# State products of the sample streams: four fp32 products of 32 rows at TensorE's row tiles, in place of six full products with masked rows

## The chip, the cores and the metric

The kernel runs on one core of one Trainium2 chip. The metric is the time of one execution in device microseconds, taken as the median of several runs; lower is better. The engines are named as the profile names them: PE is TensorE's matrix product and PEld its weight load, DVE is VectorE, ACT is ScalarE, POOL is GpSimd, and SP is the queue that issues nearly all DMAs. PSUM, where products land, has eight banks of 128 x 512 fp32 values.

## The reference

Two request groups, a prompt of 512 frames and eight sample streams of 16 frames each, pass together through two layers. In each layer a combined projection feeds a gated MLP branch and a gated DeltaNet branch, and an MLP follows. The change lies in the DeltaNet branch, where each of eight heads updates a state S of 128 x 128 per stream:

```
def step(S, xs):
    U_, W_, P_, qg_, kg_, gl_ = xs
    vnew = U_ - jnp.einsum('bhcd,bhde->bhce', W_, S)
    o = jnp.einsum('bhcd,bhde->bhce', qg_, S) + jnp.einsum('bhij,bhje->bhie', P_, vnew)
    S = S * gl_[..., None, None] + jnp.einsum('bhcd,bhce->bhde', kg_, vnew)
    return S, o
```

The prompt has one stream, taken here in four chunks of 128 frames. The samples have eight streams of 16 frames each; together they make one tile of 128 rows, in which stream b owns rows 16 b to 16 b + 15. Their state update is, per stream, the product of 16 rows of `kg` with the same 16 rows of `vnew`: eight results of 128 x 128 a head.

## The kernel before

The activations lie transposed, features on partitions and 640 frames along the free axis. A matrix product with a weight block is written as three products in fp32r: both operands are split into a high part (ScalarE's copy, L133) and a low part (VectorE's subtraction, L134), and high x high, high x low and low x high are summed. A weight block of 128 outputs is thus 16 units of three products of 320 columns; the names `pg_p` and `pg_g` in the profile are their PSUM tiles, `raw`, `whi` and `wlo` the weight block and its parts.

The DeltaNet work of a layer is spread among these units. A layer's head stage has ten slots; slot h takes a list of weight blocks (five of them, 80 units, in slots 2 to 8). Three generators run beside the blocks: `prepare` of head h - 1, `chain` of head h - 2 and `roots` of head h - 3. Each is cut by `yield` into segments, and `paced` spreads them over the slot: a generator of length L whose next segment is due at d is resumed at the first unit u of n for which d n <= u L. `chain` has the length CHAIN, `prepare` the length PREPARE = 70. At each unit `chain` comes first, then `roots`, then `prepare`, then the unit's three products. What is due after the last unit is issued at the end of the slot.

TensorE executes in exactly this program order, written out by hand. The order on the other engines comes from a planner that lists instructions by readiness and priority; `chain` has the highest priority, then `prepare` and the splits of weights.

`chain` (L629 on) does four chunks t of the prompt one after the other: a product with the state (`ps_kS`), VectorE's `y` (L732), a product `ps_w`, ScalarE's copy `w` (L680), and then the state product `ps_S`, the output products `ps_o`, VectorE's new state (L750) and ScalarE's copy `osb` (L684). Its banks have the tag "c". Beside it runs the generator `sample` for the eight streams, with banks of the tag "d", which `prepare` and `roots` use too. Of each tag there are two banks. `prepare` ends with a product of 32 small tiles into a "d" bank, `ps_Z` (L617), and begins in the next slot with transposes into "d" banks, `kt` (L516).

`sample` scales the eight old states by their decays (POOL), computes `w` for all streams, and then forms the eight updates in two halves of four streams. For each half, `w` is masked so that each of four column blocks holds only one stream's rows (`we`: four ScalarE copies for the high part, L717, and one POOL product for the low part, L718), and three products of 128 rows and 512 columns are summed into a "d" bank; VectorE adds the bank to the states (L723). The first half is issued with `ps_w` of chunk 3, the second after the outputs of chunk 3.

Of the kernel before, what the change touches and what calls it, by code (L numbers as in the profile page):

```python
# [9 lines left out]
F32 = mybir.dt.float32  # L10
# [7 lines left out]
P = 128  # L18
# [17 lines left out]

SIDE = (1, 4, 2, 2, 2, 2, 2, 2, 5, 6)

CHAIN, PREPARE, ROOTS, GATING = 66, 70, 26, 48
AHEAD = 200  # L40


def rep(ap, dim, n):

    a = ap.unsqueeze(dim)
    shape = list(a.shape)
    shape[dim] = n
    return a.to_broadcast(shape)
# [14 lines left out]
def encoder(ctx, tc, xin, wblk, wba, sct, sdelta, prow, pcol, gates, wst, bsr, convw, consts, delta0,  # L63
# [68 lines left out]
    def split(dst_hi, dst_lo, src):  # L132
        nc.scalar.activation(dst_hi, src, AF.Copy)  # L133
        nc.vector.tensor_tensor(dst_lo, src, dst_hi.bitcast(F32), op=ALU.subtract)  # L134
# [52 lines left out]
    def bank(tag, nm):  # L187
        return psp.tile([P, 512], F32, tag=tag, name=f"ps_{nm}")
# [440 lines left out]
    def chain(l, h, pl, gate, out):  # L629
        sq, kT, qg, kg, AP_, vn, n0c, QT, S8 = out.pop(h)  # L630
        beta, ngam, egam, dL, dec, rowd = gate
        kb, qb, N1 = kbs[h % 2], qbs[h % 2], n1s[h % 2]
        nm = f"{l}{h}"


        m0c = pl.tile([P, 4, 32], F32, tag="m0c", bufs=1, name=f"m0c{nm}")
        nc.vector.transpose(m0c[:].rearrange("p t n -> p (t n)"), n0c[:, 0:4, :].rearrange("p t n -> p (t n)"))
        M0 = pl.tile([P, 4, 64], F32, tag="M0", bufs=1, name=f"M0{nm}")
        N0 = pl.tile([P, 5, 64], F32, tag="N0", bufs=2, name=f"N0{nm}")
        for dst, src, n in ((M0, m0c, 4), (N0, n0c, 5)):  # L640
            for b in range(2):
                nc.vector.tensor_scalar(dst[:, :, 32 * b:32 * b + 32], src[:, 0:n, :], odd[:, b:b + 1], None, op0=ALU.mult)
        yield 8
        by = bank("c", f"Y{nm}")
        bys = by[:, 0:256].rearrange("p (t n) -> p t n", t=4)
        for t in range(4):
            for hf in halves:
                mm(bys[hf, t, :], QT[hf, t, :], M0[hf, t, :], True, True, pos=(hf.start, hf.start))
        Y = pl.tile([P, 4, 64], F32, tag="Y", bufs=1, name=f"Y{nm}")
        nc.scalar.activation(Y[:], bys, AF.Copy)  # L650
        yield 4
        b1 = bank("c", f"M1{nm}")
        for t in range(4):
            mm(b1[0:64, t * 64:(t + 1) * 64], N0[0:64, t, :], Y[0:64, t, :], True, True)
        M1 = pl.tile([P, 4, 64], F32, tag="M1", bufs=1, name=f"M1{nm}")
        nc.vector.tensor_tensor(M1[0:64], b1[0:64, 0:256].rearrange("p (t n) -> p t n", t=4), M0[0:64], op=ALU.add)
        bz = bank("c", f"Z{nm}")
        bzs = bz[:, 0:256].rearrange("p (t n) -> p t n", t=4)
        for t in range(4):
            for hf in halves:  # L660
                mm(bzs[hf, t, :], Y[hf, t, :], N0[hf, t, :], True, True, pos=(hf.start, hf.start))
        for hf in halves:
            nc.vector.tensor_tensor(N1[hf, :, hf], bzs[hf], N0[hf, 0:4, :], op=ALU.add)
        yield 5
        b2 = bank("c", f"Y2{nm}")
        for t in range(4):
            mm(b2[64:128, t * 64:(t + 1) * 64], AP_[0:64, t, 0, 64:128], M1[0:64, t, :], True, True, pos=(0, 64))
        nc.scalar.activation(M1[64:128].rearrange("p t n -> p (t n)"), b2[64:128, 0:256], AF.Copy)
        yield 4
        b3 = bank("c", f"N2{nm}")  # L670
        for t in range(4):
            mm(b3[0:64, t * 64:(t + 1) * 64], M1[64:128, t, :], N1[64:128, t, 64:128], True, True, pos=(64, 0))
        nc.vector.tensor_copy(N1[0:64, :, 64:128], b3[0:64, 0:256].rearrange("p (t n) -> p t n", t=4))
        yield 4

        osb = pl.tile([P, 5, P], F32, tag="osb", bufs=1, name=f"osb{nm}")

        def copied(ps, tag):
            tl = pl.tile([P, P], F32, tag=tag, bufs=1, name=f"{tag}{nm}")
            nc.scalar.activation(tl[:], ps, AF.Copy)  # L680
            return tl

        def o_done(po, t):
            nc.scalar.activation(osb[:, t, :], po[:, 0:P], AF.Copy)  # L684


        def sample():
            pk = bank("d", f"kS{nm}4")
            pq = bank("d", f"qS{nm}4")
            for ps, buf in ((pk, kb), (pq, qb)):  # L690
                for j in range(2):
                    for c in range(4):
                        mm(ps[32 * c:32 * c + 32, 0:P], buf[:, c, 16 * j:16 * j + 32], S8[:, 2 * c + j, :], j == 0, j == 1, pos=(0, 32 * c))
            y = pl.tile([P, P], F32, tag="y4", bufs=1, name=f"y{nm}4")
            nc.vector.scalar_tensor_tensor(y[:], pk[:, 0:P], egam[:, 4, h:h + 1], vn[:, 4, :], op0=ALU.mult, op1=ALU.add)
            qs = copied(pq[:, 0:P], "qs")
            nc.gpsimd.tensor_tensor(S8[:], S8[:], rep(dec[:, 4:12, h], 2, P), op=ALU.mult)
            yield
            pw = bank("d", f"w{nm}4")
            for hf in halves:  # L700
                mm(pw[hf, 0:P], N0[hf, 4, :], y[hf], True, True, pos=(hf.start, hf.start))
            w = copied(pw[:, 0:P], "w4")
            wp_, kp = (pl.tile([P, 2, P], F32R, tag=tag, name=f"{tag}{nm}") for tag in ("w4p", "k4p"))
            split(wp_[:, 0, :], wp_[:, 1, :], w[:])
            split(kp[:, 0, :], kp[:, 1, :], kg[:, 4, :])
            yield
            po = bank("d", f"o{nm}4")
            mm(po[:, 0:P], w[:], AP_[:, 4, 1, :], True, False)
            mm(po[:, 0:P], qs[:], ident, False, True)
            o_done(po, 4)  # L710
            yield
            Sf = S8[:].rearrange("p b n -> p (b n)")
            for a in range(2):

                we = pl.tile([P, 2, 4, P], F32R, tag="we", name=f"we{nm}{a}")
                for b in range(4):
                    nc.scalar.activation(we[:, 0, b, :], wp_[:, 0, :].bitcast(F32), AF.Copy, scale=maskb[:, 4 * a + b:4 * a + b + 1])  # L717
                nc.gpsimd.tensor_tensor(we[:, 1], rep(wp_[:, 1, :].bitcast(F32), 1, 4), rep(maskb[:, 4 * a:4 * a + 4], 2, P), op=ALU.mult)  # L718
                yield
                pS = bank("d", f"S{nm}4{a}")  # L720
                for i, (u, v) in enumerate(((0, 0), (0, 1), (1, 0))):
                    mm(pS[:], kp[:, u, :], we[:, v].rearrange("p b n -> p (b n)"), i == 0, i == 2)
                nc.vector.tensor_tensor(Sf[:, a * 512:(a + 1) * 512], Sf[:, a * 512:(a + 1) * 512], pS[:], op=ALU.add)  # L723
            nc.sync.dma_start(ds_out[l, :, h].rearrange("b d e -> d b e"), S8[:])

        beside, S = sample(), None
        for t in range(4):
            if t:
                pk = bank("c", f"kS{nm}{t}")
                mm(pk[:, 0:P], kT[:, t, :], S[:], True, True)  # L730
                y = pl.tile([P, P], F32, tag="y", bufs=1, name=f"y{nm}{t}")
                nc.vector.scalar_tensor_tensor(y[:], pk[:, 0:P], egam[:, t, h:h + 1], vn[:, t, :], op0=ALU.mult, op1=ALU.add)  # L732
                if t >= 2:
                    next(beside)
                yield 4
            pw = bank("c", f"w{nm}{t}")
            mm(pw[:, 0:P], N1[:, t, :], y[:] if t else vn[:, 0, :], True, True)
            w = copied(pw[:, 0:P], "w")
            if t:
                next(beside)  # L740
            yield 4
            pS = bank("c", f"S{nm}{t}")
            mm(pS[:, 0:P], kg[:, t, :], w[:], True, True)
            po = bank("c", f"o{nm}{t}")
            mm(po[:, 0:P], w[:], AP_[:, t, 1, :], True, t == 0)
            if t:
                mm(po[:, 0:P], S[:], qg[:, t, :], False, True)
            Sn = pl.tile([P, P], F32, tag="S", bufs=2, name=f"S{nm}{t}")
            if t:
                nc.vector.scalar_tensor_tensor(Sn[:], S[:], dec[:, t, h:h + 1], pS[:, 0:P], op0=ALU.mult, op1=ALU.add)  # L750
            else:
                nc.vector.tensor_copy(Sn[:], pS[:, 0:P])
            S = Sn
            o_done(po, t)
            if t < 3:
                yield 4
        nc.sync.dma_start(dp_out[l, h], S[:])
        run(beside)
        out[h, "o"] = osb, sq
# [611 lines left out]
```

## Time and profile before

| what | value |
|---|---|
| median of 3 runs | 2483.79 us (2483.41 to 2486.56) |
| the profiled execution: its own time | 2483.95 us |
| its span, first to last instruction | 2482.0 us |
| mean granted TensorE clock | 0.993 |
| PE busy | 2424.5 us, 98% |
| DVE, ACT, POOL busy | 60%, 49%, 19% |
| masked copies `we` | 128 on ScalarE, 32 on POOL |
| products `ps_S<-we,k4p` | 96, of 512 columns |

A row of a timeline gives the start in us from the span's start, how long the group lasted, engine, line, operation, the tile written and those read, shape and count; in square brackets, where there are any, stand the engine's idle time before it and what ended it. TensorE's products overlap in their pipeline, so its pace is read from one start to the next. An fp32 product appears as two records.

### The profile page before, as it was taken

The page shows a single profiled execution, that of the slowest core. Times are in us where ns is not written, and L with a number is a line of the kernel's source. Part 1 is how long each engine was busy: PE and PEld are TensorE (multiplying, and loading weights), DVE is VectorE, ACT ScalarE, POOL GpSimd, SP SyncE. Part 2 cuts the span into 40 slices and gives each one's busy share as a digit, 9 for nine tenths or more (in the row PEclk, how much of TensorE's full clock was granted, in tenths as well). Part 3 has the DMA queues.
Part 4 walks back from the last instruction along what each step waited for, and adds up shares of the span by engine and source line. Part 5 has one row for each costly group of instructions (what it writes and reads, how often), then busy time and mean ns, then how long its engine had stood idle before and what let it go on. Part 6 is the DMA issues. An engine that isn't in the chain of part 4 may idle for free. (4 is left out here: it accounts for less than half of the span.)

```text
span 2482.0 us, 44959 instructions
## 1 busy us (share of the span) xinstructions
PE 2424.5 (98%) x18120; PEld 2338.1 (94%) x18120; DVE 1477.9 (60%) x2982; ACT 1212.8 (49%) x2324; POOL 482.1 (19%) x582
## 2 busy tenths in 40 slices
PE   8999999999999999999999999999999999999997
PEld 7999999998999999999999999999989999999997
DVE  6656677536555746556456677664275567556453
ACT  5767676633123625244447676774332245244352
POOL 0223433211222100000213343341112220000002
PEclk9999999999999999999999999999999999999998
DMA  5233333337532222222233333333464322222221
GB/s 175 86 108 115 111 92 95 126 115 243 160 104 77 69 77 85 69 86 77 85 95 117 102 97 97 102 117 114 153 226 139 98 65 81 69 85 77 78 83 61
DMA packets 124495, 261.27 MB, mean 105 GB/s; under 512 B 17232, under 2 KB 57072, under 8 KB 124288
## 3 DMA queue, kind: packets, MB, share of 16 engines
q1 hardware_dynamic: 123968, 257.10, 32.2%
q8 instruction: 142, 2.33, 0.4%
q0 software_dynamic: 320, 1.31, 0.2%
q14 instruction: 65, 0.53, 0.1%
HBM read 218.22 MB, written 40.15 MB: 104 GB/s over the span
## 5 line engine op out<-in xcount | busy, mean ns | idle before, releaser
L133 ACT ACTIVATE whi<-raw 128x1024 fp32r<-128x1024 f32 (+1 forms) x304 | 309.0, 1018 | 630.6 <-PE pg_dn L80 255.4
L134 DVE TENSOR_TENSOR wlo<-raw,whi 128x1024 fp32r<-128x1024 f32 (+1 forms) x304 | 383.7, 1263 | 171.0 <-ACT whi L133 157.2
L80 PE MATMUL pg_dn<-gh,wlo 128*128 128x320 f32 x1024 | 317.3, 310 | 2.1 <-DVE wlo L134 2.1
L80 PE MATMUL pg_dn<-gl,whi 128*128 128x320 f32 x1024 | 316.6, 309 | 0.7 <-DVE gl L1128 0.7
L80 PE MATMUL pg_dn<-gh,whi 128*128 128x320 f32 x1024 | 316.8, 309 | 0.0
L80 PE MATMUL pg_g<-Ah,whi 128*128 128x320 f32 x896 | 289.4, 323 | 1.0 <-ACT sg L830 1.0
L80 PE MATMUL pg_g<-Ah,wlo 128*128 128x320 f32 x896 | 276.8, 309 | 0.0
L80 PE MATMUL pg_g<-Al,whi 128*128 128x320 f32 x896 | 276.4, 308 | 0.0
L80 PE MATMUL pg_p<-Ah,whi 128*128 128x320 f32 x768 | 251.4, 327 | 0.0
L80 PE MATMUL pg_p<-Al,whi 128*128 128x320 f32 x768 | 236.9, 309 | 0.4 <-DVE Al L134 0.4
L80 PE MATMUL pg_p<-Ah,wlo 128*128 128x320 f32 x768 | 237.2, 309 | 0.0
L80 PEld LDWEIGHTS pg_dn<-gh,wlo 128*128 128x128 f32 x1024 | 192.2, 188 | 4.4 <-DVE wlo L134 4.4
L80 PEld LDWEIGHTS pg_dn<-gl,whi 128*128 128x128 f32 x1024 | 192.2, 188 | 1.2 <-DVE gl L1128 1.2
L80 PEld LDWEIGHTS pg_dn<-gh,whi 128*128 128x128 f32 x1024 | 192.2, 188 | 0.0
L80 PEld LDWEIGHTS pg_g<-Ah,whi 128*128 128x128 f32 x896 | 168.6, 188 | 8.7 <-issue 3.5
L1242 DVE TENSOR_TENSOR t<-pg_dn,rateb 128x640 f32<-128x640 f32 x64 | 52.7, 824 | 202.5 <-PE pg_dn L80 202.5
L80 PEld LDWEIGHTS pg_g<-Al,whi 128*128 128x128 f32 x896 | 168.7, 188 | 1.5
L80 PEld LDWEIGHTS pg_g<-Ah,wlo 128*128 128x128 f32 x896 | 168.2, 188 | 0.0
L479 DVE SCALAR_TENSOR_TENSOR yb<-cb,cw,yb 128x664 f32<-128x664 f32 x144 | 138.1, 959 | 27.4 <-ACT yb L477 25.8
L80 PEld LDWEIGHTS pg_p<-Ah,whi 128*128 128x128 f32 x768 | 145.2, 189 | 6.0 <-issue 2.4
L80 PEld LDWEIGHTS pg_p<-Al,whi 128*128 128x128 f32 x768 | 144.7, 188 | 0.7 <-DVE Al L134 0.7
L80 PEld LDWEIGHTS pg_p<-Ah,wlo 128*128 128x128 f32 x768 | 144.2, 188 | 0.0
(748 smaller groups left out, 6245.3 us busy)
## 6 DMA issues: line engine op xcount, KB each, us to landing
raw<-in_wblk SPq DMA_DIRECT2D x304, 512.0 KB, 3.5
gd<-sg SPq DMA_DIRECT2D x56, 320.0 KB, 3.3
rg<-gd SPq DMA_DIRECT2D x44, 320.0 KB, 3.2
S<-in_sdelta SPq DMA_DIRECT2D x16, 512.0 KB, 6.1
out<-S SPq DMA_DIRECT2D x16, 512.0 KB, 3.8
gr<-rowd SPq DMA_DIRECT2D x16, 320.0 KB, 5.2
er<-rowd SPq DMA_DIRECT2D x16, 320.0 KB, 3.9
ond<-osb SPq DMA_DIRECT2D x16, 320.0 KB, 2.2
```

The source lines that it names most:

```text
L80: nc.tensor.matmul(out, lhsT=lhsT, rhs=rhs, start=start, stop=stop, **kw)
L133: nc.scalar.activation(dst_hi, src, AF.Copy)
L134: nc.vector.tensor_tensor(dst_lo, src, dst_hi.bitcast(F32), op=ALU.subtract)
L479: nc.vector.scalar_tensor_tensor(yb[:, 0:CY], cb[:, j:j + CY], cw[:, c, j:j + 1], yb[:, 0:CY], op0=ALU.mult, op1=ALU.add)
L1242: nc.vector.tensor_tensor(t[:], ps[:, :, 0:HT], rate, op=ALU.mult)
```

## The change

The split of `w` and `kg` for the samples goes, and with it the masks by stream. Instead ScalarE writes two copies of `w`, one that keeps the even streams and one that keeps the odd ones (`par` holds one for the rows of even or of odd streams, zero for the others). Rows 32 c to 32 c + 31 hold streams 2 c and 2 c + 1, so four products with 32 rows each, at the row tiles of the array, with 256 columns (even copy, odd copy) give the eight updates in plain fp32. Each of the four writes a bank of its own, two of tag "c" and two of tag "d", and four VectorE additions of 256 columns take them up.

All four products now stand in one last segment of `sample`, which runs after the outputs of chunk 3 and a further `yield 4`. The length CHAIN grows by four to match.

```diff
-CHAIN, PREPARE, ROOTS, GATING = 66, 70, 26, 48
+CHAIN, PREPARE, ROOTS, GATING = 70, 70, 26, 48
...
             w = copied(pw[:, 0:P], "w4")
-            wp_, kp = (pl.tile([P, 2, P], F32R, tag=tag, name=f"{tag}{nm}") for tag in ("w4p", "k4p"))
-            split(wp_[:, 0, :], wp_[:, 1, :], w[:])
-            split(kp[:, 0, :], kp[:, 1, :], kg[:, 4, :])
+
+            w2 = pl.tile([P, 2, P], F32, tag="w2", bufs=1, name=f"w2{nm}")
+            for j in range(2):
+                nc.scalar.activation(w2[:, j, :], w[:], AF.Copy, scale=par[:, j:j + 1])
             yield
             po = bank("d", f"o{nm}4")
             mm(po[:, 0:P], w[:], AP_[:, 4, 1, :], True, False)
             mm(po[:, 0:P], qs[:], ident, False, True)
             o_done(po, 4)
             yield
-            Sf = S8[:].rearrange("p b n -> p (b n)")
-            for a in range(2):
-
-                we = pl.tile([P, 2, 4, P], F32R, tag="we", name=f"we{nm}{a}")
-                for b in range(4):
-                    nc.scalar.activation(we[:, 0, b, :], wp_[:, 0, :].bitcast(F32), AF.Copy, scale=maskb[:, 4 * a + b:4 * a + b + 1])
-                nc.gpsimd.tensor_tensor(we[:, 1], rep(wp_[:, 1, :].bitcast(F32), 1, 4), rep(maskb[:, 4 * a:4 * a + 4], 2, P), op=ALU.mult)
-                yield
-                pS = bank("d", f"S{nm}4{a}")
-                for i, (u, v) in enumerate(((0, 0), (0, 1), (1, 0))):
-                    mm(pS[:], kp[:, u, :], we[:, v].rearrange("p b n -> p (b n)"), i == 0, i == 2)
-                nc.vector.tensor_tensor(Sf[:, a * 512:(a + 1) * 512], Sf[:, a * 512:(a + 1) * 512], pS[:], op=ALU.add)
+            yield
+            yield
+            banks = [bank(tag, f"S{nm}4{c}") for c, tag in enumerate("ccdd")]
+            for c, q in enumerate(quarters):
+                mm(banks[c][:, 0:2 * P], kg[q, 4, :], w2[q].rearrange("p b n -> p (b n)"), True, True, pos=(q.start, 0))
+            for c in range(4):
+                nc.vector.tensor_tensor(S8[:, 2 * c:2 * c + 2, :], S8[:, 2 * c:2 * c + 2, :],
+                                        banks[c][:, 0:2 * P].rearrange("p (b n) -> p b n", b=2), op=ALU.add)
             nc.sync.dma_start(ds_out[l, :, h].rearrange("b d e -> d b e"), S8[:])
...
             o_done(po, t)
-            if t < 3:
-                yield 4
+            yield 4
         nc.sync.dma_start(dp_out[l, h], S[:])
         run(beside)
```

## The prediction

> **What bounds the kernel now.** I read the page first, then the windows of single head slots, then the timelines of TensorE, VectorE and ScalarE around the products that the diff touches.
>
> ```profile
> span 2482.0 us, 44959 instructions
> PE 2424.5 (98%) x18120; PEld 2338.1 (94%) x18120; DVE 1477.9 (60%) x2982; ACT 1212.8 (49%) x2324; POOL 482.1 (19%) x582
> L1242 DVE TENSOR_TENSOR t<-pg_dn,rateb 128x640 f32<-128x640 f32 x64 | 52.7, 824 | 202.5 <-PE pg_dn L80 202.5
> ```
>
> ```profile
> 191.20:243.00 51.80, 51.80 (x478) 48.84 (x478) 35.81 (x116) 36.12 (x89) 20.31 (x30) 1.00 0.34 105
> 243.00:294.80 51.80, 51.80 (x478) 48.84 (x478) 35.99 (x116) 36.12 (x89) 20.34 (x30) 1.00 0.35 106
> ```
>
> The second fence is the windows view: time, then busy time of PE, PEld, DVE, ACT and POOL, then clock and DMA. Two head slots in a row last 51.80 us each with PE busy in all of it, at full granted clock, while DVE and ACT have some 16 us free. So TensorE sets the end of this stage, in the order in which its instructions are written. An edit there is worth what it adds to or takes from TensorE's own time, plus any wait that it plants in TensorE's queue. Busy time does not show short waits (the ends are modelled), so I read start to start.
>
> The sum is made against the profiled execution, 2483.95 us: its span of 2482.0 and 1.95 around it. The median of the runs is 2483.79, 0.16 below.
>
> **Removed: the six products.** First an fp32 product followed by the stream (PE timeline, one piece), then the slot's end with the second stretch of three.
>
> ```profile
> 182.63 0.38 PE L80 MATMUL ps_kS<-S,kT 128*128 128x128 f32 x2
> 182.77 0.39 PE L80 MATMUL pg_g<-Ah,whi 128*128 128x320 f32 x1
> 183.00 0.30 PE L80 MATMUL pg_g<-Al,whi 128*128 128x320 f32 x1
> ```
>
> ```profile
> 188.30 0.38 PE L80 MATMUL ps_S<-w,kg 128*128 128x128 f32 x2
> 188.52 0.39 PE L80 MATMUL ps_o<-AP,w 128*128 128x128 f32 x2
> 188.74 0.39 PE L80 MATMUL ps_o<-qg,S 128*128 128x128 f32 x2
> 188.88 0.95 PE L80 MATMUL ps_S<-we,k4p 128*128 128x512 f32 x3
> 189.67 0.31 PE L80 MATMUL pg_g<-Ah,whi 128*128 128x320 f32 x1
> 189.82 0.31 PE L80 MATMUL pg_g<-Al,whi 128*128 128x320 f32 x1
> 189.97 0.31 PE L80 MATMUL pg_g<-Ah,wlo 128*128 128x320 f32 x1
> 190.21 0.45 PE L80 MATMUL ps_Z<-n0c,y 32*32 32x32 f32 x32
> 190.61 0.66 PE L516 MATMUL ps_kt02a<-cst,kT 128*128 128x128 f32 x4
> 191.17 0.33 PE L516 MATMUL ps_kt02b<-cst,kT 128*128 128x128 f32 x1
> ```
>
> From an fp32 product to the second stream product it takes 183.00 - 182.63 = 0.37 us; with three products of 512 columns between, 189.82 - 188.74 = 1.08. So a stretch costs 0.71, and two stretches in each of 16 heads 22.7 us.
>
> **Added: four fp32 products at row tiles.** No product of the trace uses four row tiles over all 128 columns. The nearest are four column tiles (`ps_kS`, `ps_qS`) and two diagonal tiles of 64 rows (`ps_w<-y,N`).
>
> ```profile
> 219.72 0.62 PE L80 MATMUL ps_qS<-S,qb 128*32 128x128 f32 x16
> 220.27 0.42 PE L80 MATMUL pg_p<-Ah,whi 128*128 128x320 f32 x1
> ```
>
> ```profile
> 225.44 0.38 PE L80 MATMUL ps_kS<-S,kT 128*128 128x128 f32 x2
> 225.75 0.44 PE L80 MATMUL ps_w<-y,N 64*64 64x128 f32 x4
> 226.12 0.42 PE L80 MATMUL pg_g<-Ah,whi 128*128 128x320 f32 x1
> 226.37 0.31 PE L80 MATMUL pg_g<-Al,whi 128*128 128x320 f32 x1
> ```
>
> An fp32 product is two records, and one of 128 columns takes 188.52 - 188.30 = 0.22, so 0.11 a pass. Sixteen records of `ps_qS` fit into 0.55 us where one after the other they would take 1.76: tiles run side by side. The two-tile group costs 226.37 - 225.44 - 0.37 = 0.56, of which two passes are 0.22; 0.34 is the drain in, an uncovered weight load, the drain out and another load. The load back to 128 columns is 226.37 - 226.12 - 0.15 = 0.10, so entering with 128 columns of weights instead of 64 adds 0.05. Two passes of 256 columns are 0.44, and the tiles' starts are spread over 0.02. Sum 0.85 a head, 13.6 us. Upper end: no overlap at all between row tiles, 4 x 0.44 instead of 0.44, 1.30 more a head. Lower end: no fixed cost, 0.44. I take 0.85, because both tiled groups of the trace overlap.
>
> "TensorE: Matmul & The Clock Gate", Part 3, of the Trainium skill gives a measured speedup of 3.07 for four row tiles instead of 4. By that, an estimate, a pass takes 1.30 times as long, 0.13 us a head and 2.1 us in all, and the sum below would end at 2495. No run here shows row tiles of this kind yet.
>
> **Where it stands, and the bank it takes.** In slots 2 to 8 (80 units of three stream products) a segment due at d is issued at unit ceil(80 d / CHAIN). The state products, due at 65 of 66 and now 69 of 70, are at unit 79 in both. One unit later, at the slot's end, `prepare` issues its last product `ps_Z` (L617), which needs a "d" bank. Before, only one "d" bank was in use by then. Now two of the four new banks are "d" and there are only two, so `ps_Z` waits for the third of four VectorE adds, and with it everything that TensorE has behind it: the transposes `kt` and the next slot's stream.
>
> ```profile
> 189.87 0.69 DVE L723 TENSOR_TENSOR S<-S,ps_S 128x512 f32<-128x512 f32 x1 [0.80 <-PE ps_S L80]
> 190.47 0.45 DVE L134 TENSOR_TENSOR k4p<-kg,k4p 128x128 fp32r<-128x128 f32 x1
> 190.84 0.28 DVE L618 TENSOR_TENSOR n0c<-n0c,ps_Z 128x128 f32<-128x128 f32 x1
> ```
>
> Let P be the last stream start ahead of the group. The group starts at P + 0.24 (190.21 - 189.97), its second pass at P + 0.58 (0.22 + 0.10 + 0.02). A 128-column record lasts 0.27 (0.38 less 0.11), so one of 256 lasts 0.38 and ends at P + 0.96. The add follows after 0.04 (188.88 + 0.95 to 189.87). An add of 512 columns lasts 0.69 and the next starts after 0.60; 640 columns last 0.824. So 256 columns last 0.42 and follow each other by 0.33: the third ends at P + 1.00 + 0.66 + 0.42 = P + 2.08, and TensorE goes on 0.05 later (190.56 to 190.61), P + 2.13. Without the wait `ps_Z` would start at P + 0.58 + 0.31 + 0.25 + 0.15 + 0.24 = P + 1.53. The wait is 0.60 in each of 14 heads (slots 2 to 8 of two layers), 8.4 us. Ends: 0 if that bank comes free within the unit, and 1.9 if a 1.23 us VectorE split is put among the adds. "TensorEngine Tiling (Array Packing)", PSUM Bottleneck, of the Trainium skill speaks against the change in the same way: tiling hastens TensorE, not the emptying of PSUM.
>
> A credit: the add after `ps_Z` was held by the split of `k4p` until 190.84, and `kt02b` started 0.18 after the last `kt02a` where 0.11 is its pace; `k4p` goes, so 0.07 x 14 = 1.0 us returns.
>
> **Moved: the chain, earlier by up to four units.** CHAIN 70 puts `kS` of chunk 2 (due 45) at unit 52 instead of 55 and `ps_w` of chunk 2 with the sample's `ps_o` (due 49) at 56 instead of 60. What feeds them on VectorE and ScalarE does not move with them.
>
> ```profile
> 226.40 1.23 DVE L134 TENSOR_TENSOR wlo<-raw,whi 128x1024 fp32r<-128x1024 f32 x1 [2.29 <-ACT whi L133]
> 227.54 0.34 DVE L732 SCALAR_TENSOR_TENSOR y<-ps_kS,cu,vtok 128x128 f32<-128x128 f32 x1
> ```
>
> ```profile
> 223.72 1.28 ACT L499 ACT_TABLE_LOAD   x1 [3.04 <-DVE pr L591]
> 225.33 1.04 ACT L133 ACTIVATE whi<-raw 128x1024 fp32r<-128x1024 f32 x1
> 228.43 0.26 ACT L680 ACTIVATE w<-ps_w 128x128 f32<-128x128 f32 x1
> ```
>
> ```profile
> 228.27 0.31 PE L80 MATMUL pg_g<-Ah,wlo 128*128 128x320 f32 x1
> 228.41 0.38 PE L80 MATMUL ps_w<-y,n 128*128 128x128 f32 x2
> 228.74 0.49 PE L80 MATMUL ps_o<-AP,w 128*128 128x128 f32 x2
> 229.06 0.39 PE L80 MATMUL ps_o<-cst,qs 128*128 128x128 f32 x2
> ```
>
> ```profile
> 1658.81 0.34 DVE L732 SCALAR_TENSOR_TENSOR y<-ps_kS,cu,vtok 128x128 f32<-128x128 f32 x1
> ```
>
> `y` stands behind `wlo`, which waits for `whi`, which stands on ScalarE behind a table load for `E`, which waits for VectorE's substitution of another head. `y` ends at 227.88, half a microsecond before TensorE wants it. Four units earlier (12 products at 13 steps in 1.90 us, 226.37 to 228.27, so 1.76) TensorE is there at 226.65. If the order `E`, `whi`, `wlo`, `y` stays, it waits until 227.94: 1.29 us. The wait for `w` that `ps_o` had (229.06 - 228.41 is 0.65 where four records take 0.44, so 0.21) is swallowed. Net 1.08 a head, in the ten heads with this pattern (slots 3 to 7 of both layers, the first `y` at 227.54, the last at 1658.81): 10.8 us. Ends: 0 if `y` goes ahead of `wlo`, 1.66 if `w`, ending at 228.69, decides (`ps_o` at 228.74 instead of 226.87, less the 0.21).
>
> **Edits at nothing.** ScalarE loses eight masked copies and two splits a head and gets two scaled copies, POOL loses two, VectorE has four shorter adds for two:
>
> ```profile
> L717 ACT ACTIVATE we<-w4p,mis x128: 384/389/410, 176.5 to 1764.9; 128x128 fp32r<-128x128 f32 x128
> L718 POOL TENSOR_TENSOR we<-w4p,mis x32: 1037/1042/1049, 176.8 to 1764.1; 128x512 fp32r<-128x512 f32 x32
> L723 DVE TENSOR_TENSOR S<-S,ps_S x32: 686/689/689, 185.8 to 1767.1; 128x512 f32<-128x512 f32 x32
> ```
>
> ScalarE gives back 6 x 0.39 x 16 = 37 us and POOL 33 us, beside TensorE's stream; VectorE's adds take 4 x 0.42 instead of 2 x 0.69. Were that cover gone, VectorE's 0.3 us a head would cost 5 us. The store of the states is issued on SP's queue after the last add, as before, at about the same time; behind it stand only loads for blocks two ahead. In slot 9 chain and roots now fill 96 of 96 units instead of 92; no `prepare` follows, so no bank wait.
>
> **Sum.** -22.7 + 13.6 + 8.4 - 1.0 + 10.8 = +9.1 on 2483.95: 2493.
>
> **The rivals.** First, no mid-slot wait: scheduling places `y` ahead of `wlo`, or `whi` ahead of `E`. VectorE idles 2.29 us ahead of `wlo`, which speaks for it; against it, the due times move the chain alone, while `E`, `whi` and `wlo` are issued where they were. Then -1.7: 2482.3, no change. Second, on the other side, TensorE's saving stands bare, because the adds of the two "d" banks are done first: `ps_Z` then waits for the first add, P + 1.00 + 0.42 + 0.05 = P + 1.47, before it is due. Its place is the slot's end, its price 8.4 us; with the first rival it gives -10.1, 2474, and it decides once the bank is back by P + 1.53. For it: VectorE idles 0.80 ahead of that add. Against: program order, "c" before "d". Third, the row tiles do not overlap: +20.8, and the bank wait goes since the adds start tile by tile; 2494.7, or 2505.5 with the mid-slot wait. Against it: every tiled group seen overlaps, though each uses other columns.
>
> **How the numbers follow.** Forecast 0.42, first rival 0.27, second 0.22, third 0.09. About 0.2% (5 us) can be told from no change. Slower: forecast and third less a share with a smaller wait, 0.50; within: 0.28; faster: 0.22. The range runs from the second rival, 2474 (2473 with a little for rounding), to the third with the wait, 2506; the forecast's own is 2488 to 2501 (waits of 0.6 to 1.66, bank waits as worked out).
>
> **What would show it.** Products `ps_S<-w2,kg` starting four within 0.03 us and two passes 0.32 apart: tiles overlap. `ps_Z` some 0.6 us late behind the third add: the bank wait. `ps_w` of chunk 2 behind `y` and `wlo` in slots 3 to 7: the mid-slot wait. A slot of 51.80 us becoming 52.8 is the forecast, 51.8 the first rival, 51.2 the second, 52.5 the third. It is wrong if the engines' order changes with the due times.

## The result, and the profile after

The changed kernel takes 2496.07 us (median of 4 runs, 2494.12 to 2499.57) where the kernel before took 2483.73 beside it: ratio 1.0052, 95% interval 1.0038 to 1.0066. The change costs 12.3 us. The forecast was 2493, slower by 9.1. The profiled execution is the slowest of the four (2499.57 us, span 2497.9), so I take from it lengths of slots and of waits, and not the span.

First the page of the kernel after: span, and busy time of the engines.

```profile
span 2497.9 us, 44813 instructions
PE 2419.2 (97%) x18152; PEld 2327.5 (93%) x18152; DVE 1479.8 (59%) x2982; ACT 1164.6 (47%) x2184; POOL 436.8 (17%) x550
```

TensorE's busy time fell by 5.3 us, ScalarE's by 48, POOL's by 45, and the kernel became slower. So the loss lies in TensorE's waits. One head slot in the windows view (from the first transpose `kt` of one slot to that of the next) shows the same:

```profile
192.19:245.21 53.02, 51.27 (x488) 47.99 (x479) 36.37 (x115) 32.90 (x80) 17.00 (x27) 1.00 0.33 102
```

It lasts 53.02 us where the slot before lasted 51.80, and PE is busy for only 51.27 of it: 1.75 us are now idle time that the view can see. Slots 3 to 7 all have this length, to 0.01 us, in both layers. Slot 2 went from 51.17 to 51.99, slot 8 from 51.50 to 51.56, slot 9 from 54.64 to 54.10. Over both layers the slots 2 to 9 add up to +12.5 us, which is the difference of the medians.

The end of a slot, TensorE's timeline of the kernel after:

```profile
189.70 0.31 PE L80 MATMUL pg_g<-Ah,wlo 128*128 128x320 f32 x1
189.94 0.71 PE L80 MATMUL ps_S<-w,kg 32*128 32x256 f32 x8
190.58 0.41 PE L80 MATMUL pg_g<-Ah,whi 128*128 128x320 f32 x1
190.83 0.31 PE L80 MATMUL pg_g<-Al,whi 128*128 128x320 f32 x1
190.98 0.31 PE L80 MATMUL pg_g<-Ah,wlo 128*128 128x320 f32 x1
191.81 0.45 PE L80 MATMUL ps_Z<-n0c,y 32*32 32x32 f32 x32 [0.52 <-DVE S L719]
192.19 0.66 PE L516 MATMUL ps_kt02a<-cst,kT 128*128 128x128 f32 x4
192.69 0.33 PE L516 MATMUL ps_kt02b<-cst,kT 128*128 128x128 f32 x1
```

The four products and their two passes (eight records) start within 0.34 us, and the second stream product behind them follows the last one ahead of them by 190.83 - 189.70 = 1.13; two normal steps are 0.29, so the group costs 0.84. `ps_Z` was due 0.24 after 190.98, at 191.22, and starts at 191.81: 0.59 late, held by `S`. VectorE's timeline there:

```profile
190.67 1.42 DVE L719 TENSOR_TENSOR S<-S,ps_S 128x256 f32<-128x256 f32 x4 [3.06 <-PE ps_S L80]
192.34 0.29 DVE L618 TENSOR_TENSOR n0c<-n0c,ps_Z 128x128 f32<-128x128 f32 x1 [0.25 <-PE ps_Z L80]
```

The four adds start 0.33 apart and last 0.42; the third ends at 190.67 + 0.66 + 0.42 = 191.75, and `ps_Z` starts 0.06 later.

The middle of the slot: TensorE, then VectorE, then ScalarE.

```profile
228.12 0.31 PE L80 MATMUL pg_g<-Ah,wlo 128*128 128x320 f32 x1
229.66 0.46 PE L80 MATMUL ps_w<-y,n 128*128 128x128 f32 x2 [1.23 <-DVE y L729]
...
230.18 0.39 PE L80 MATMUL ps_o<-cst,qs 128*128 128x128 f32 x2
```

```profile
224.93 0.17 DVE L591 TENSOR_TENSOR pr<-Bs,X 128x5 f32<-128x5 f32 x1
...
228.02 1.22 DVE L134 TENSOR_TENSOR wlo<-raw,whi 128x1024 fp32r<-128x1024 f32 x1 [2.46 <-ACT whi L133]
229.16 0.34 DVE L729 SCALAR_TENSOR_TENSOR y<-ps_kS,cu,vtok 128x128 f32<-128x128 f32 x1
```

```profile
225.18 1.28 ACT L499 ACT_TABLE_LOAD   x1 [3.77 <-DVE pr L591]
226.48 0.40 ACT L499 ACTIVATE E<-gr,ngam 128x128 f32<-128x128 f32 x1
...
226.94 1.05 ACT L133 ACTIVATE whi<-raw 128x1024 fp32r<-128x1024 f32 x1
```

`ps_w` of chunk 2 was due one step after 228.12, at 228.27, and starts at 229.66: 1.39 us in which TensorE stands with the stream queued behind it. Read upwards, it is the chain that the prediction named: `y` behind `wlo`, `wlo` waiting for `whi`, `whi` behind the table load and `E`, and that load waiting for the last product `pr` of VectorE's substitution. (The next head's `E` has only one buffer, and the substitution's `Bs` lies in it until `pr` has read it.) Counted from start to start there are 12 such waits of `ps_w` with 14.8 us in all: ten of 1.39 in slots 3 to 7, and two of 0.44 in slot 2, where it is the product of chunk 3.

### The profile page after: what moved, and what is told of

Same layout as the page of the kernel before. It is cut to its first block, busy times and chain, and to the rows that moved or that the text cites. A ratio compares the mean times of both kernels' runs of the same rounds, so it can differ in the third digit from the quotient of the medians.

```text
span 2497.9 us, 44813 instructions
## 1 busy us (share of the span) xinstructions
PE 2419.2 (97%) x18152; PEld 2327.5 (93%) x18152; DVE 1479.8 (59%) x2982; ACT 1164.6 (47%) x2184; POOL 436.8 (17%) x550
## 5 line engine op out<-in xcount | busy, mean ns | idle before, releaser
L479 DVE SCALAR_TENSOR_TENSOR yb<-cb,cw,yb 128x664 f32<-128x664 f32 x144 | 145.2, 1008 | 24.5 <-ACT yb L477 23.3
```

The lines of the kernel that those rows point to most:

```text
L479: nc.vector.scalar_tensor_tensor(yb[:, 0:CY], cb[:, j:j + CY], cw[:, c, j:j + 1], yb[:, 0:CY], op0=ALU.mult, op1=ALU.add)
```

## The experiments

My theory: the new products are cheap, and the loss is two waits. One comes with the length CHAIN (TensorE reaches `ps_w` four units earlier, `y` does not move), the other with the order of the banks ("c" before "d"). The main rival: the row-tile products themselves cost more than they save, and the later or earlier places are innocent. Ratios are against the kernel before, run on the same chip; its medians there were 2485.59 (first four kernels below) and 2484.88 us (the next three), and 2482.88 for the last.

**The old products at the new pace.** The kernel before with only the length changed:

```diff
-CHAIN, PREPARE, ROOTS, GATING = 66, 70, 26, 48
+CHAIN, PREPARE, ROOTS, GATING = 70, 70, 26, 48
```

> The kernel before with one number changed, CHAIN 70 instead of 66: the six masked products stay, the chain's segments come up to four units earlier. Theory (the due times plant a wait behind y and wlo in slots 3 to 7): ps_w of chunk 2 waits for y some 1.1 to 1.3 us in ten heads, so 10.8 to 12.5 us slower than before, 2494.5 to 2496. Rival (the time is lost in the four new products, their adds and their banks): no change, 2483.7.

It took 2515.18 us, 1.0128 (1.0114 to 1.0142). The mid-slot wait came without any row tile: 12 waits, 16.1 us. So that wait belongs to the pace. But the kernel lost some 30 us instead of the 10.8 to 12.5 expected, by a second wait that I had not foreseen (TensorE's timeline of this kernel, at the end of a slot):

```profile
240.73 0.39 PE L80 MATMUL ps_o<-AP,w 128*128 128x128 f32 x2
240.95 0.39 PE L80 MATMUL ps_o<-qg,S 128*128 128x128 f32 x2
242.86 0.96 PE L80 MATMUL ps_S<-we,k4p 128*128 128x512 f32 x3 [1.52 <-ACT we L717]
```

The second stretch of the old products now comes before ScalarE has made its masked copies `we`: 12 times, 18.5 us in all, 1.77 where it is shown (242.86 - 240.95, where the kernel before takes 0.14). Together the two waits are more than the loss by the medians, by some 5 us; the difference lies outside the head slots, and I did not assign it. The new products have no copies of that length ahead of them, and no such wait. So the lengths 66 and 70 are not an edit that can be judged apart from the products: at 70 the old products do far worse than the new ones.

**The "d" banks added first.** On the changed kernel:

```diff
-            banks = [bank(tag, f"S{nm}4{c}") for c, tag in enumerate("ccdd")]
+            banks = [bank(tag, f"S{nm}4{c}") for c, tag in enumerate("ddcc")]
```

> The changed kernel with the four banks taken in the order d, d, c, c instead of c, c, d, d, so that ps_Z has to wait for the first add and not for the third. Theory (a bank wait of 0.59 us in 14 heads): ps_Z starts without a wait, 8.3 us faster than the changed kernel, about 2487.8; the mid-slot wait stays. Rival (row-tiled products and their switches cost more than they save, whatever the bank): 2496, no gain.

2492.89 us, 1.0032 (1.0020 to 1.0045). `ps_Z` no longer waits, in any head, so the order of the banks is its cause. But the slot only fell from 53.02 to 52.67, by 0.35 and not by 0.59. TensorE and VectorE at the slot's end:

```profile
242.78 0.31 PE L80 MATMUL pg_g<-Ah,wlo 128*128 128x320 f32 x1
243.01 0.45 PE L80 MATMUL ps_Z<-n0c,y 32*32 32x32 f32 x32
243.40 0.66 PE L516 MATMUL ps_kt03a<-cst,kT 128*128 128x128 f32 x4
244.13 0.33 PE L516 MATMUL ps_kt03b<-cst,kT 128*128 128x128 f32 x1
```

```profile
242.47 1.42 DVE L719 TENSOR_TENSOR S<-S,ps_S 128x256 f32<-128x256 f32 x4 [3.06 <-PE ps_S L80]
243.80 0.28 DVE L618 TENSOR_TENSOR n0c<-n0c,ps_Z 128x128 f32<-128x128 f32 x1
```

`kt03b` starts 0.73 after `kt03a` where 0.50 is its pace. The add `n0c`, which empties the bank of `ps_Z`, stands behind all four adds on VectorE (without idle time ahead of it, where it had 0.25 before), and the next transposes need that bank. So 0.23 of the 0.59 came back one instruction later, at the next user of the bank that `ps_Z` has.

**The old pace.** On the changed kernel, the chain's places put back, by taking the added steps from chunk 3:

```diff
-CHAIN, PREPARE, ROOTS, GATING = 70, 70, 26, 48
+CHAIN, PREPARE, ROOTS, GATING = 66, 70, 26, 48
...
-                yield 4
+                yield 4 if t < 3 else 3
...
-            yield 4
+            yield 4 if t < 3 else 3
...
-            yield 4
+            yield 4 if t < 2 else 3
```

> The changed kernel with CHAIN back at 66 and the yields of chunk 3 and the last one of chunk 2 cut from 4 to 3, so that the first three chunks keep the old pace and the four products still come at unit 79. Theory: the wait of ps_w of chunk 2 goes (10 x 1.25 us), the bank wait at ps_Z stays (14 x 0.59): about 2483.5 to 2485, as the kernel before. Rival (the wait comes from something else than the due times, or returns at chunk 3, whose steps are now 3.6 units apart): 2490 to 2496.

2486.33 us, 1.0004 (0.9995 to 1.0013): no longer slower than before. The mid-slot wait is gone, and the slots are 52.03 us long. Two places on TensorE and one on VectorE:

```profile
235.25 0.31 PE L80 MATMUL pg_g<-Ah,wlo 128*128 128x320 f32 x1
235.67 0.49 PE L80 MATMUL ps_kS<-S,kT 128*128 128x128 f32 x2
...
236.14 0.31 PE L80 MATMUL pg_g<-Al,whi 128*128 128x320 f32 x1
...
243.43 0.31 PE L80 MATMUL pg_g<-Ah,wlo 128*128 128x320 f32 x1
244.26 0.45 PE L80 MATMUL ps_Z<-n0c,y 32*32 32x32 f32 x32 [0.52 <-DVE S L719]
```

```profile
235.27 0.34 DVE L747 SCALAR_TENSOR_TENSOR S<-S,dec,ps_S 128x128 f32<-128x128 f32 x1
```

What is left are the bank wait (7.6 us in 14 heads) and a small new one: chunk 3 starts one step earlier, and its first product `ps_kS` waits for VectorE's new state. It starts 0.42 after the stream product ahead of it, where 0.15 is the pace, and the second stream product behind it follows 0.47 after that, where 0.37 is (its second pass starts 0.21 after the first and not 0.11, as in other products that have waited). That is 0.37 in each of ten heads, 3.7 us.

**Both.** The two edits above together:

> Both edits together: old pace of the first three chunks, and the banks in the order d, d, c, c. Theory: both waits gone, the bare saving of 0.56 us a head is left: 2496 - 12.5 - 8.3 = about 2475, faster than the kernel before by 8 to 9 us. Rival (the waits only move): no faster than 2483.

2480.47 us, 0.9982 (0.9973 to 0.9991), with slots of 51.67 us. The change is now a gain of some 5 us. I had counted on 8 to 9; what is missing lies in the two small waits of the runs above, 0.24 at `kt` and 0.37 at `ps_kS`, in ten heads each.

**Chunk 3 paced further on.** As the last, but with the step taken from the end of chunk 3:

```diff
-            yield 4 if t < 2 else 3
+            yield 4 if t < 3 else 2
```

> As e4 (banks d, d, c, c; CHAIN 66), but the last yield of chunk 2 is 4 again and those of chunk 3 are 3, 3, 2, so that ps_kS of chunk 3 keeps its old unit 70. Theory (the 0.24 us that ps_kS of chunk 3 waits in e3 and e4 comes from its being two units early): that wait goes, 12 x 0.24 = 2.9 us less than e4, about 8 us faster than the kernel before. Rival: the wait turns up at ps_w or ps_S of chunk 3, whose units are closer now, and nothing is won.

2478.74 us, 0.9978 (0.9969 to 0.9987), with slots of 51.31: the wait of `ps_kS` is gone in slots 3 to 7, the one at `kt` stays. The interval overlaps that of the last run; the slots tell the two apart, by 0.36, and that is the wait of `ps_kS` with its late second pass.

**Three adds on VectorE.** As the last, but the fourth bank is copied by ScalarE and added by POOL, so that `n0c` stands behind three adds:

```diff
-                nc.vector.tensor_tensor(S8[:, 2 * c:2 * c + 2, :], S8[:, 2 * c:2 * c + 2, :],
-                                        banks[c][:, 0:2 * P].rearrange("p (b n) -> p b n", b=2), op=ALU.add)
+                s, ps = S8[:, 2 * c:2 * c + 2, :], banks[c][:, 0:2 * P].rearrange("p (b n) -> p b n", b=2)
+                if c == 3:
+                    up = pl.tile([P, 2, P], F32, tag="up", bufs=1, name=f"up{nm}")
+                    nc.scalar.activation(up[:], ps, AF.Copy)
+                    nc.gpsimd.tensor_tensor(s, s, up[:], op=ALU.add)
+                else:
+                    nc.vector.tensor_tensor(s, s, ps, op=ALU.add)
```

> As e7 (below), and the fourth add is taken off VectorE: ScalarE copies that bank to SBUF and POOL adds it, so that the add after ps_Z is not queued behind four adds. Theory (the 0.24 us that kt waits in e2 is VectorE's queue of adds): kt follows ps_Z at its own pace, 0.24 less a head than e7, 14 x 0.24 = 3.4 us; about 11 us faster than the kernel before. Rival (ps_Z's own add is late for another reason): as e7.

2472.81 us, 0.9959 (0.9946 to 0.9971): 12.1 us faster than the kernel before, and faster than both kernels. Windows, TensorE, VectorE:

```profile
239.96:291.02 51.06, 51.06 (x488) 48.01 (x478) 34.79 (x115) 33.15 (x80) 19.59 (x29) 1.00 0.34 107
```

```profile
239.96 0.66 PE L516 MATMUL ps_kt03a<-cst,kT 128*128 128x128 f32 x4
240.46 0.33 PE L516 MATMUL ps_kt03b<-cst,kT 128*128 128x128 f32 x1
```

```profile
239.03 1.08 DVE L725 TENSOR_TENSOR S<-S,ps_S 128x256 f32<-128x256 f32 x3 [1.61 <-PE ps_S L80]
240.11 0.29 DVE L618 TENSOR_TENSOR n0c<-n0c,ps_Z 128x128 f32<-128x128 f32 x1
```

`n0c` starts at 240.11, within the `kt` group, and `kt03b` follows at its pace of 0.50. PE is busy through the whole slot again, as it was before the change. This also answers the main rival: the row-tile products, with their waits gone, save what the sum of removed and added work says (-22.7 + 13.4 = -9.3). Slots 2 to 9 of both layers are together 10.7 us shorter than in the kernel before: 9.3 by the products, and 1.4 by small delays of the kernel before at `kt` and at the `ps_kS` of chunk 3 that are gone as well. The other 1.4 by the medians lie outside these slots.

**`E` moved out of the way of `whi`.** To see what holds the mid-slot chain, on the changed kernel at its own pace: the decays of the next head are issued behind the copy `y32`, and their bias depends on it, so that the table load comes later.

```diff
-            nc.scalar.activation(E[:, t, :], er[:, t, :], AF.Exp, bias=gate[1][:, h, t:t + 1])
+            nc.scalar.activation(E[:, t, :], er[:, t, :], AF.Exp, bias=gate[1][:, h, t:t + 1] if nb is None else nb[:, t:t + 1])
...
-        if h + 1 < H:
-            decays(l, h + 1, pl, gate, er, out)
...
+        if h + 1 < H:
+            nb = pl.tile([P, 5], F32, tag="nb", bufs=1, name=f"nb{nm}")
+            nc.vector.scalar_tensor_tensor(nb[:], y32[:, 0, 0:5], 0.0, ngam[:, h + 1, :], op0=ALU.mult, op1=ALU.add)
+            decays(l, h + 1, pl, gate, er, out, nb)
```

> The changed kernel with CHAIN 70 kept, and one thing moved: the exponentials E of the next head, which held whi up on ScalarE, get a bias that depends on y32, the copy of ps_Y at unit 76, so they can't stand ahead of whi of unit 48. Theory (y is late because wlo waits for whi, and whi stands behind E's table load, which waits for VectorE's substitution): whi, wlo and y come some 2 us earlier in the slot, the wait of ps_w of chunk 2 (14.8 us in all) goes, and the kernel is about as fast as the one before, unless E's burst at the slot's end makes something else late. Rival (y is late by the due times alone, whatever stands ahead of whi): still 10 to 12 us slower than before.

2491.73 us, 1.0034 (1.0022 to 1.0047). The mid-slot waits fell from 14.8 to 5.5 us, not to nothing. Of the 9.3 so won some 4 came back in other places, about half of them as waits of `ps_kS` in a few heads; the rest I did not assign. ScalarE, VectorE, TensorE:

```profile
222.08 0.62 ACT L598 ACTIVATE n0c<-X,par 128x80 f32<-128x80 f32 x2 [3.93 <-DVE X L594]
...
222.76 1.05 ACT L133 ACTIVATE whi<-raw 128x1024 fp32r<-128x1024 f32 x1
```

```profile
223.84 1.23 DVE L134 TENSOR_TENSOR wlo<-raw,whi 128x1024 fp32r<-128x1024 f32 x1 [0.79 <-ACT whi L133]
224.98 0.35 DVE L730 SCALAR_TENSOR_TENSOR y<-ps_kS,cu,vtok 128x128 f32<-128x128 f32 x1
```

```profile
224.86 0.31 PE L80 MATMUL pg_g<-Ah,wlo 128*128 128x320 f32 x1
225.47 0.46 PE L80 MATMUL ps_w<-y,n 128*128 128x128 f32 x2 [0.30 <-ACT yb L477]
```

The chain `whi`, `wlo`, `y`, `ps_w` is the same, 0.93 us earlier; `ps_w` waits 225.47 - 224.86 - 0.15 = 0.46. (The bracket names another releaser, but `y` ends at 225.33, 0.14 ahead.) With `E` out of the way `whi` stood behind the copies `n0c`, which wait for the same substitution `X`. So the table load is a part of the wait, and behind both lies the substitution on VectorE. (A second buffer for `E`, which would free the table load from `pr`, was not run.)

**No scaling on POOL.** What makes the substitution late? In the kernel after, one of its small operations is ten times as long as its neighbours, and it lies beside POOL's scaling of the old states (VectorE, then POOL):

```profile
221.20 0.18 DVE L591 TENSOR_TENSOR pr<-Bs,X 128x30 f32<-128x30 f32 x1
221.41 1.79 DVE L594 TENSOR_TENSOR X<-X,pr 128x30 f32<-128x30 f32 x1
```

```profile
221.18 1.98 POOL L697 TENSOR_TENSOR S<-S,dec 128x1024 f32<-128x1024 f32 x1 [0.22 <-PE ps_qS L80]
```

The kernel before has the same, and `y` was early enough there to hide it (VectorE, then POOL):

```profile
220.51 1.89 DVE L591 TENSOR_TENSOR pr<-Bs,X 128x20 f32<-128x20 f32 x1
```

```profile
220.45 1.92 POOL L697 TENSOR_TENSOR S<-S,dec 128x1024 f32<-128x1024 f32 x1 [0.22 <-PE ps_qS L80]
```

So the scaling was taken off POOL and fused into the adds, on the changed kernel at its own pace:

```diff
-            nc.gpsimd.tensor_tensor(S8[:], S8[:], rep(dec[:, 4:12, h], 2, P), op=ALU.mult)
...
-            for c in range(4):
-                nc.vector.tensor_tensor(S8[:, 2 * c:2 * c + 2, :], S8[:, 2 * c:2 * c + 2, :],
-                                        banks[c][:, 0:2 * P].rearrange("p (b n) -> p b n", b=2), op=ALU.add)
+            for c in range(8):
+                nc.vector.scalar_tensor_tensor(S8[:, c, :], S8[:, c, :], dec[:, 4 + c, h:h + 1],
+                                               banks[c // 2][:, c % 2 * P:c % 2 * P + P], op0=ALU.mult, op1=ALU.add)
```

> The changed kernel with the scaling of the old states taken off POOL: eight fused VectorE operations (state times decay plus update, 128 columns each) in place of POOL's scaling and the four adds. Theory: VectorE's substitution, on which ScalarE's queue ahead of `whi` hangs, is late because one of its operations takes 1.8 to 1.9 us instead of 0.2 while POOL scales the states. Then that long operation is gone, `whi`, `wlo` and `y` come up to 1.7 us earlier, and the mid-slot wait of `ps_w` falls from 1.39 us to near 0 (14.8 us in all to under 2). The bank wait grows, since six operations of 0.34 us, some 0.25 apart, now stand ahead of the third bank's release instead of three adds 0.33 apart: from 0.59 to about 1.1, +7 us in 14 heads. Together 2496 - 14 + 7, about 2489, a ratio near 1.002; slots 3 to 7 near 52.1 us. Rival: POOL has nothing to do with the long operation. Then it stays, the mid-slot wait stays 1.39, the bank wait still grows, and the kernel takes about 2503 (ratio 1.008, slots of 53.5 us).

2490.42 us, 1.0028 (1.0019 to 1.0038), with slots of 52.26. All 12 mid-slot waits are gone, at the length 70. VectorE and TensorE:

```profile
219.47 0.19 DVE L594 TENSOR_TENSOR X<-X,pr 128x30 f32<-128x30 f32 x1
...
225.63 0.34 DVE L728 SCALAR_TENSOR_TENSOR y<-ps_kS,cu,vtok 128x128 f32<-128x128 f32 x1
```

```profile
226.18 0.31 PE L80 MATMUL pg_g<-Ah,wlo 128*128 128x320 f32 x1
226.32 0.38 PE L80 MATMUL ps_w<-y,n 128*128 128x128 f32 x2
...
242.06 0.45 PE L80 MATMUL ps_Z<-n0c,y 32*32 32x32 f32 x32 [1.17 <-DVE S L718]
```

The same operation takes 0.19 us, `y` starts 1.67 earlier in its slot and ends at 225.97, and `ps_w` follows the stream without a gap. The price is at the slot's end, as expected in kind: `ps_Z` stands behind six of eight longer operations and waits 1.24 us a head, 17.3 in all where it was 8.3, and the transposes another 0.13. The rival (POOL has no part in it) would have kept the mid-slot wait and given 2503; it falls.

## Why the prediction was right

Taken term by term:

- **Removed products, -22.7.** Slot 9, which has neither wait, bears it out: -0.54 measured, where 0.84 - 1.42 gives -0.58.
- **Added products, +13.6.** 0.84 a head instead of 0.85, so 13.4. The four row tiles overlap: the next stream product starts 190.58 - 189.94 = 0.64 after the group's start, where four products one after the other would take 4 x 0.44. The third rival fell with it. The estimate of 2.1 us more, worked out from a figure of "TensorE: Matmul & The Clock Gate", Part 3, of the Trainium skill (given there for 512 columns), is not borne out for these four fp32 products of 32 rows and 256 columns: the group costs no more than the sum without it.
- **Bank wait, +8.4.** 0.59 a head, 8.3 in 14 heads. The second rival (the "d" banks' adds come first by themselves) did not happen; made to happen, it gave only 0.35 of the 0.59, since the rival's working stopped at `ps_Z` and did not go on to the add that empties its bank. "TensorEngine Tiling (Array Packing)", PSUM Bottleneck, of the Trainium skill says that tiling hastens TensorE and not the emptying of PSUM; the trace agrees, with 0.59 us a head of waiting at the next user of the banks.
- **Credit at `kt`, -1.0.** `kt02b` starts 0.50 after `kt02a` instead of 0.56. That is 0.06, and in 12 heads, not 14 (slot 9 has no transposes): -0.7.
- **Mid-slot wait, +10.8.** The mechanism and the order `E`, `whi`, `wlo`, `y` stood, and the first rival fell. Its root I had not seen: the substitution at the head of that order is late by the 1.6 us that VectorE loses beside POOL's scaling, before the change as after it. The size was off. I let TensorE go on 0.06 after `y` ends; it took 229.66 - 229.50 = 0.16, so each wait is 1.39 and not 1.29. What it swallows is smaller than the 0.21 I took off: from `ps_w` to the second `ps_o` it took 0.65 before (228.41 to 229.06) and takes 230.18 - 229.66 = 0.52 now, since a product that has waited sends its second pass 0.18 after the first and not 0.11. The net is 1.39 - 0.13 = 1.26 a head, where I had 1.08. And slot 2, which I left out, loses 0.83 in each layer, at `ps_w` of chunk 3 and at `ps_o` of chunk 2. In all 12.6 + 1.7 = +14.3.

The new sum is -22.7 + 13.4 + 8.3 - 0.7 + 14.3 = +12.6, against 12.5 by the slots and 12.3 by the medians. The 3 us that the forecast was short are in the last term.

The bounds were not all worked out as said. With the mid-slot wait at its upper end of 1.66 the sum gives 2499 and not 2501; the upper end of the bank wait (0.60 + 1.23 is 1.83, not 1.9) would have given some 2510, outside the 2506 at which I closed the range. No run had that case.

The forecast slot was 52.8 and the measured one 53.02. What the experiments add is that both waits sit in how the products are placed and not in the products.

## What to carry to other kernels

When one engine executes in written order, price a cheaper operation and its new place as two edits: here the operation saved 9 to 10 us and its place lost 22 to 23. Before moving a consumer earlier by some units, read what its producer stands behind on the other engines, up to the first operation that is longer than its neighbours; before taking more banks at once, ask who needs those banks next, and go on to the instruction that empties that one's bank too.

## What the runs showed of the hardware

Four fp32 row tiles of 32 rows and 128 columns ran side by side: their four starts lie within 0.02 us of each other, and the second pass of each follows 0.32 after its first (eight starts in 0.34, less the spread of 0.02). 256 columns at the fp32 pace of 0.11 us for 128 are 0.22 of that; how the rest divides between loading weights and a cost of sharing, no run shows. What a group costs beside its two passes, 0.84 - 0.44 = 0.40 us, is nearly as much as the work in it.

A small VectorE operation that runs into POOL's scaling of 128 x 1024 values is stretched from 0.2 to about 1.8 us and ends just after POOL's work does (223.20 against 223.16 in the rows above). It happens in 12 heads of the changed kernel and of the kernel before. With that scaling gone, no operation of the substitution takes more than 0.28 us. The page "SBUF — State Buffer", 🔬 SBUF: two separate sides, of the Trainium skill says that VectorE and GpSimd share a pair of ports as an exclusive lock, which a VectorE operation with two SBUF inputs needs against a GpSimd operation that reads SBUF, and that the loser waits for the whole instruction. The rows agree: `X<-X,pr` has two SBUF inputs, and it is held to the end of POOL's 1.98 us. One row shows that the hold does not begin with POOL's record: the `pr` ahead of it, also with two inputs in SBUF, starts 0.02 after POOL's scaling and takes its usual 0.18, while in the kernel before a `pr` that starts 0.06 after it is held. In slot 8 a transpose with one SBUF input runs beside the scaling and takes its usual 0.31. Had I laid that sentence beside the substitution before predicting, the root of the late `y` would have been in reach.
